# Token tiles handed from one part of a network to the next in a written-out order

## The chip, the cores and the metric

The kernel runs on one core of a Trainium2 chip. The metric is the device time of one execution, in microseconds (us). A core has a matrix engine (PE, with its weight loads as PEld), a vector engine (DVE), a scalar engine (ACT), a general engine (POOL) and an engine that only issues transfers (SP). Each engine runs its own instructions in the order in which they stand in its stream, and waits on semaphores for the others.

## The reference

Two layers, each of three parts; x is 512 tokens by 1024 channels, in float32:

```
x = x + 0.5 * rms(FFN1(rms(x) * g_pre)) * g_post     # SwiGLU, width 2816
x = x +       rms(MIXER(rms(x) * g_pre)) * g_post    # attention + convolution + linear attention, gated, projected
x = x + 0.5 * rms(FFN2(rms(x) * g_pre)) * g_post
```

So there are six parts, and five times the output of one part, still in the accumulators, has to be normed, scaled by `g_post`, added to x, normed again, scaled by `g_pre` and transposed before the next part can multiply with it. This passage is what the change touches.

## The kernel before, in words

Tokens are tiled by 128 into four tiles. Every product is made from three matmuls, because each operand is split into a high part (rounded by ACT, `hi` or `h`) and a low part (the difference, by DVE, `lo` or `l`): high x high, high x low, low x high. `split` (line 111) is that pair; the weights are loaded by SP into `raw` and split into `whi` and `wlo` (lines 112 and 113, of which there are five buffers each).

An FFN multiplies by seven half-size products instead of eight (`block_tiles`, then `Down` for the down projection). `Down.run` (line 614) goes through its products step by step, with weights asked for four steps ahead; after the third product it calls `late` (line 640), which fetches the next two norm weights, `g_post` of this part and `g_pre` of the next (`load_g`, line 188: one row broadcast to 128 partitions, 512 KB).

`out_proj` (line 258) ends every part. All but the last four steps of the contraction are accumulated for all tokens first. The last four (`rest`) are then run token tile by token tile: token 0, 1, 2, 24 matmuls of 512 columns each, and token 3. Two accumulators, one for each half of the channels, are thus complete after each 12 matmuls. After each token `finish` is called. It runs `post_norm` (line 239), that is

- for an FFN, `Down.results` (line 657), which adds or subtracts the taps kept from the seven products;
- `rms` (line 197): two squares with a sum on ACT, a mean on DVE (`ms`), a power on POOL (`rs`);
- two scalings by `g_post` on DVE (`tn`, line 244), which free the accumulators, and two adds to x (line 248);

and `pre_norm` (line 210): `rms` again, on x, then two scalings by `rs` and `g_pre` into `hn` on DVE (line 220). For tiles 0 and 1 the second half is instead multiplied by `g_pre` on POOL (line 214) and scaled by `rs` on ACT (line 218).

`pre_norm` returns `arrive`, which is called later: eight transposes on PE (line 71), a split into `xh` and `xl` (lines 112, 113), and before an FFN the copies `xr` and the sums and differences T that the seven products need. Tile 0's `arrive` is called after the first quarter of token 3's matmuls. Those of tiles 1 to 3 are called by the next part: in the middle of the product of the tile before (mixer, `pv`, line 780) or between its gate and up halves (FFN, `pf`, lines 701 to 705).

`early` fetches the first weights of the next part in four steps. The first step is taken before token 0, the other three after token 3's matmuls are written. The mixer's first product takes two of its eight contraction blocks from each step; the FFN's gate takes the first two steps and its up half the other two.

What sets the order: matmuls and transposes are pinned, and so is all of `block_tiles` and `Down`. A pinned instruction (`tc.keep_in_program_order`, line 68) stays behind everything that the program wrote before it on its engine. Everything else is placed by a planner, which picks what it takes to be ready, earlier lines first. In the kernel before all of `post_norm`, `pre_norm`, `arrive`, the early weights' splits and `load_g` are left to the planner.

Of the kernel before, what the change touches and what calls it, by code (L numbers as in the profile page):

```python
# [13 lines left out]
P = 128  # L14
D = 1024
# [26 lines left out]
def kernel(  # L42
# [58 lines left out]
    def room(n, dt=F32R):  # L101
        cur[n] = resid.tile([P, KC, S], dt, tag=n, name=n)
        return cur[n]
# [4 lines left out]
        nc.sync.dma_start(x_sb[i], x_in[0, i * P:(i + 1) * P, :])  # L108


    def split(hi, lo, src):
        nc.scalar.copy(hi, src)  # L112
        nc.vector.tensor_tensor(lo, src, hi.bitcast(F32), op=ALU.subtract)  # L113

    spare = []

# [70 lines left out]

    def load_g(row):
        g = gp.tile([P, D], F32, tag="g", name="g")
        nc.sync.dma_start(g, row.unsqueeze(0).broadcast_to([P, D]))  # L190
        return g

    def rsqrt_eps(dst, src, n):
# [16 lines left out]
    def pre_norm(i, gB, pooled=(), forms=None):  # L210
        t = slice(i * P, (i + 1) * P)
        hns = [slot("hn", tag="b") for j in range(2)]
        for j in pooled:
            nc.gpsimd.tensor_tensor(hns[j], x_sb[i][:, HS[j]], gB[:, HS[j]], op=ALU.mult)
        rs = rms([x_sb[i][:, c] for c in HS])
        for j in range(2):
            if j in pooled:
                nc.scalar.mul(hns[j], hns[j], rs)
            else:
                nc.vector.scalar_tensor_tensor(hns[j], x_sb[i][:, HS[j]], rs, gB[:, HS[j]], op0=ALU.mult, op1=ALU.mult)  # L220

        def arrive():
            if i == 0:
                room("xh")
                room("xl")
            pts = []
            for j, hn in enumerate(hns):
                pt = bank("pt")
                for k in range(4):
                    transpose(pt[:, k * P:(k + 1) * P], hn[:, k * P:(k + 1) * P], ident)  # L230
                src = pt.rearrange("p (k t) -> p k t", t=P)
                split(cur["xh"][:, 4 * j:4 * j + 4, t], cur["xl"][:, 4 * j:4 * j + 4, t], src)
                pts.append(src)
            if forms is not None:
                forms.arrive(i, pts)

        return arrive

    def post_norm(i, banks, gB, factor):
        rs = rms(banks)  # L240
        tn = []
        for h in range(2):
            t = slot("tn", tag="s")
            nc.vector.scalar_tensor_tensor(t, banks[h], factor, gB[:, HS[h]], op0=ALU.mult, op1=ALU.mult)
            tn.append(t)
        for h in range(2):
            x = x_sb[i][:, HS[h]]
            nc.vector.scalar_tensor_tensor(x, tn[h], rs, x, op0=ALU.mult, op1=ALU.add)  # L248

    def load_rows(w2d, k):  # L250
        return load_w([(lambda r: r, w2d[k * P:(k + 1) * P, :])], 1024)
# [6 lines left out]
    def out_proj(w2d, nk, stat, tail, finish, upcoming, early, head=None):  # L258


        ld = lambda k: load_rows(w2d, k)
        fresh = head is None
        if fresh:
            banks = [[bank(f"o{i}{h}", "pb" if i < 3 else "pa") for h in range(2)] for i in range(NT)]
        else:
            banks, rest = head

        def mms(i, h, k, sh, sl, wh, wl):
            mm_out(banks[i][h], slice(i * P, (i + 1) * P), sh, sl, wh[:, HS[h]], wl[:, HS[h]],
                   fresh and k == 0, k == nk - 1)  # L270

        for k in range(nk - tail if fresh else 0):
            wh, wl = ld(k)
            sh, sl = stat(k)
            for i in range(NT):
                for h in range(2):
                    mms(i, h, k, sh, sl, wh, wl)
        if fresh:
            rest = [(k, ld(k), stat(k)) for k in range(nk - tail, nk)]
        w = None  # L280
        if early is not None:
            w, steps = early()
            next(steps)
        for i in range(NT - 1):
            for h in range(2):
                for k, (wh, wl), (sh, sl) in rest:
                    mms(i, h, k, sh, sl, wh, wl)
            finish(i, banks[i])

        for n, (k, (wh, wl), (sh, sl)) in enumerate(rest):  # L290
            for h in range(2):
                mms(NT - 1, h, k, sh, sl, wh, wl)
            if upcoming and n == tail // 2 - 2:
                upcoming[0]()
        if w is not None:
            for _ in steps:
                pass
        finish(NT - 1, banks[NT - 1])
        return w


# [178 lines left out]
    class Down:  # L480
# [173 lines left out]
                rest.append((self.steps[p][1], (hi, lo), (sh, sl)))  # L654
            return self.out, rest

        def results(self, i, banks):

            tt = nc.vector.tensor_tensor
            if i >= 2:  # L660
                tt(self.p1[i - 2], banks[0], self.p1[i - 2], op=ALU.add)
                return [self.p1[i - 2], banks[1]]
            tt(self.u2[i], banks[0], self.u2[i], op=ALU.subtract)
            tt(self.u4[i], banks[1], self.u4[i], op=ALU.add)
            return [self.u2[i], self.u4[i]]


    def ffn_weights(wg, wu):
# [12 lines left out]
    def ffn(wg, wu, wd, weights, forms, arrive, finish, upcoming, early, late, begin):  # L681

        if begin is None:
            wgt, wut = weights
        else:
            wgt = load_kcols(wg, 0, 256)
            begin(0)
            wut = load_kcols(wu, 0, 256)
            begin(1)
            arrive[0]()  # L690
        hk = []
        hid = [None] * NF

        def silu_up(i, pf):
            h = slot("ht", tag="s")
            nc.scalar.activation(h[:, 0:256], pf[:, 0:256], AF.Silu)
            nc.vector.tensor_tensor(h[:, 0:256], pf[:, 256:512], h[:, 0:256], op=ALU.mult)
            hk.append(h)

        for i in range(NT):  # L700
            pf = bank("pf", "pb")
            mm_tok(pf[:, 0:256], i, wgt)
            if i + 1 < NT:
                arrive[i + 1]()
            mm_tok(pf[:, 256:512], i, wut, first=False)
            if i + 1 < NT:
                silu_up(i, pf)

        pts = []

        def between(g):

            if g == -6:
                sides.append(load_cols(wg, 2 * P))
                forms.finish("T3")
            if g == -5:
                silu_up(NT - 1, pf)
                sides.append(load_cols(wu, 2 * P))
                pg = bank("pg")
                mm_cols(pg, *sides[0])  # L720
                for f in range(2):
                    pt = bank("pth", "pa")
                    for i in range(NT):
                        transpose(pt[:, i * P:(i + 1) * P], hk[i][:, f * P:(f + 1) * P], ident)
                    pts.append(pt)
                pu = bank("pu")
                mm_cols(pu, *sides[1])
                pts.extend((pg, pu))
            if g == -4:
                forms.finish("T2")  # L730
            if g == -2:
                forms.finish("T1")
                for f in range(2):
                    hid[f] = slot("hid", tag="q")
                    pinned(nc.scalar.copy(hid[f], pts[f]))
            if g == -1:
                hid[2] = slot("hid")
                pinned(nc.scalar.activation(hid[2], pts[2], AF.Silu))
            if g == 0:
                forms.finish("T4")  # L740
            if g == 1:
                pinned(nc.vector.tensor_tensor(hid[2], pts[3], hid[2], op=ALU.mult))
                for f in range(3, NF):
                    hid[f] = slot("hid", tag="t" if f < 18 else "q")
                down.pairs()

            u, j = divmod(g, 7)
            if j in (2, 4) and u > 0:
                down.sum_tokens(fs[u - 1], j // 4)
            if g in (n - 5, n - 3, n - 1):  # L750
                down.ahead()

        sides = []
        spare.clear()
        fs = list(range(3, NF))
        n = 7 * len(fs)
        down = Down(wd, hid)
        block_tiles(wg, wu, fs, forms, hid, between)
        head = down.run(late)
        return out_proj(wd, NF, None, TAIL, lambda i, b: finish(i, down.results(i, b)), upcoming, early, head)  # L760


    def mixer(l, wv, arrive, finish, upcoming, early):
# [521 lines left out]
    for idx, (l, s) in enumerate(subs):  # L1285
# [10 lines left out]
        here, forms = forms, Forms() if s != 0 else None  # L1296
        ahead = forms

        def finish(i, banks, ahead=ahead):
            post_norm(i, banks, norms[0], 1.0 if s == 1 else 0.5)  # L1300
            if len(norms) > 1:
                upcoming.append(pre_norm(i, norms[1], (1,) if i < 2 else (), ahead))
            else:
                for h in range(2):
                    nc.sync.dma_start(out[0, i * P:(i + 1) * P, HS[h]], x_sb[i][:, HS[h]])

        early = None
        if idx + 1 < len(subs):
# [40 lines left out]
```

## Time and profile before

| | us |
|---|---|
| median of three runs | 2348.26 (2348.12 to 2349.34) |
| the profiled execution | 2348.53 |
| its span, first to last instruction | 2346.8 |
| PE busy | 2314.0 |
| DVE busy | 1850.4 |
| ACT busy | 1225.1 |
| POOL busy | 178.4 |

In the profile's rows, `out<-in` names what an instruction writes and reads, by the program's names; `L112` is line 112. A row of instructions has its start, its length and, in brackets, the idle time of its engine just before it and what ended that. A matmul's end is modelled: one of 512 columns is shown 0.39 long, though the next is issued 0.23 later. `c`, `o` and the like are the accumulators: `oA` to `oD` of the down projection, `o` of the mixer's output, `pv` and `pf` of the next part's first product. The granted clock is the share of full speed at which PE was let run.

### The profile page before, as it was taken

The page shows a single profiled execution, that of the slowest core. Times are in us where ns is not written, and L with a number is a line of the kernel's source. Part 1 is how long each engine was busy: PE and PEld are TensorE (multiplying, and loading weights), DVE is VectorE, ACT ScalarE, POOL GpSimd, SP SyncE. Part 2 cuts the span into 40 slices and gives each one's busy share as a digit, 9 for nine tenths or more (in the row PEclk, how much of TensorE's full clock was granted, in tenths as well). Part 3 has the DMA queues.
Part 4 walks back from the last instruction along what each step waited for, and adds up shares of the span by engine and source line. Part 5 has one row for each costly group of instructions (what it writes and reads, how often), then busy time and mean ns, then how long its engine had stood idle before and what let it go on. Part 6 is the DMA issues. An engine that isn't in the chain of part 4 may idle for free. (4 is left out here: it accounts for less than half of the span.)

```text
span 2346.8 us, 36172 instructions
## 1 busy us (share of the span) xinstructions
PE 2314.0 (99%) x14072; PEld 2060.0 (88%) x14072; DVE 1850.4 (79%) x2745; ACT 1225.1 (52%) x2380; POOL 178.4 (8%) x287
## 2 busy tenths in 40 slices
PE   8999999999999999999999999999999999999998
PEld 7999887887888899997899997788878888999977
DVE  7888987859975388889788889778599644888896
ACT  5565655644323265566555566566433233565663
POOL 0000001211021100000000000012010211000000
PEclk9999999999999999999999999999999999999999
DMA  5333643231333223336423336441413322333462
GB/s 172 93 107 109 215 161 110 63 94 55 109 90 101 88 73 106 100 101 222 155 74 108 109 117 219 132 118 54 113 45 101 107 90 81 89 100 101 129 213 98
DMA packets 332764, 265.33 MB, mean 113 GB/s; under 512 B 12746, under 2 KB 285164, under 8 KB 332592
## 3 DMA queue, kind: packets, MB, share of 16 engines
q1 hardware_dynamic: 332592, 263.02, 36.8%
q8 instruction: 110, 1.80, 0.3%
q14 instruction: 62, 0.51, 0.1%
HBM read 260.88 MB, written 2.10 MB: 112 GB/s over the span
## 5 line engine op out<-in xcount | busy, mean ns | idle before, releaser
L366 DVE TENSOR_TENSOR wlo<-raw,whi 128x1024 fp32r<-128x1024 f32 (+1 forms) x304 | 331.2, 1089 | 108.7 <-ACT whi L364 108.0
L364 ACT CAST whi<-raw 128x512 fp32r<-128x512 f32 x532 | 315.4, 620 | 160.1 <-DVE raw L366 160.1
L112 ACT CAST whi<-raw 128x1024 fp32r<-128x1024 f32 (+2 forms) x178 | 185.5, 1045 | 353.2 <-PE gate L66 131.0
L113 DVE TENSOR_TENSOR wlo<-raw,whi 128x1024 fp32r<-128x1024 f32 (+2 forms) x178 | 223.1, 1262 | 168.7 <-ACT whi L112 161.9
L366 DVE TENSOR_TENSOR raw<-raw 128x512 f32<-128x512 f32 x304 | 209.3, 689 | 5.8
L66 PE MATMUL A<-xh,whi 128*128 128x256 f32 x608 | 172.5, 284 | 0.0
L66 PE MATMUL A<-xh,wlo 128*128 128x256 f32 x608 | 172.0, 283 | 0.0
L66 PE MATMUL A<-xl,whi 128*128 128x256 f32 x608 | 172.0, 283 | 0.0
L939 DVE SCALAR_TENSOR_TENSOR y<-u,cw,y 128x511 f32<-128x511 f32 (+14 forms) x240 | 166.8, 756 | 0.0
L579 ACT CAST whi<-raw 128x1024 fp32r<-128x1024 f32 x104 | 109.6, 1053 | 81.1 <-issue 36.0
L66 PE MATMUL gate<-xh,whi 128*128 128x512 f32 x384 | 151.3, 394 | 0.0
L66 PE MATMUL gate<-xh,wlo 128*128 128x512 f32 x384 | 149.8, 390 | 1.3 <-DVE wlo L113 1.3
L66 PE MATMUL gate<-xl,whi 128*128 128x512 f32 x384 | 149.6, 390 | 0.0
L582 DVE TENSOR_TENSOR wlo<-raw,whi 128x1024 fp32r<-128x1024 f32 x104 | 127.8, 1229 | 24.8 <-ACT whi L579 24.8
L205 POOL TENSOR_TENSOR rs<-ms,mhalf 128x1 f32<-128x1 f32 x48 | 28.2, 587 | 1441.2 <-DVE ms L203 1441.2
L66 PE MATMUL oA<-wlo,dh 128*128 128x512 f32 x304 | 119.7, 394 | 7.0 <-DVE wlo L582 7.0
L364 ACT COPY cp<-A 128x256 f32<-128x256 f32 x228 | 84.5, 370 | 70.6 <-PE A L66 69.7
L66 PE MATMUL oA<-whi,dl 128*128 128x512 f32 x304 | 118.4, 390 | 0.0
L66 PE MATMUL oA<-whi,dh 128*128 128x512 f32 x304 | 118.4, 389 | 0.0
L66 PEld LDWEIGHTS A<-xl,whi 128*128 128x128 f32 x608 | 116.6, 192 | 0.2
L66 PEld LDWEIGHTS A<-xh,whi 128*128 128x128 f32 x608 | 116.5, 192 | 0.2
L66 PEld LDWEIGHTS A<-xh,wlo 128*128 128x128 f32 x608 | 116.6, 192 | 0.0
(326 smaller groups left out, 7116.6 us busy)
## 6 DMA issues: line engine op xcount, KB each, us to landing
raw<-in_ffn_w_down_dram SPq DMA_DIRECT2D x152, 512.0 KB, 4.6
raw<-in_w_in_dram SPq DMA_DIRECT2D x108, 512.0 KB, 4.6
raw<-in_ffn_w_gate_dram SPq DMA_DIRECT2D x152, 256.0 KB, 3.4
raw<-in_ffn_w_up_dram SPq DMA_DIRECT2D x152, 256.0 KB, 4.5
raw<-in_w_branch_dram SPq DMA_DIRECT2D x24, 512.0 KB, 3.6
raw<-in_w_out_dram SPq DMA_DIRECT2D x16, 512.0 KB, 4.0
raw<-in_ffn_w_gate_dram SPq DMA_DIRECT2D x12, 512.0 KB, 4.9
raw<-in_ffn_w_up_dram SPq DMA_DIRECT2D x12, 512.0 KB, 4.6
```

The costliest lines, as they stand in the source:

```text
L66: tc.keep_in_program_order(nc.tensor.matmul(*a, **k))
L112: nc.scalar.copy(hi, src)
L113: nc.vector.tensor_tensor(lo, src, hi.bitcast(F32), op=ALU.subtract)
L205: nc.gpsimd.tensor_tensor(rs, ms, mhalf[:, 0:1], op=ALU.pow)
L364: copy = lambda o, i: pin(nc.scalar.copy(o, i))
L366: tt = lambda o, a, b, op: pin(nc.vector.tensor_tensor(o, a, b, op=op))
L579: pinned(nc.scalar.copy(hi, src))
L582: pinned(nc.vector.tensor_tensor(lo, src, hi.bitcast(F32), op=ALU.subtract))
L939: nc.vector.scalar_tensor_tensor(y[:, back:], u[:, :S - back], cw[:, c, j:j + 1], y[:, back:], op0=ALU.mult, op1=ALU.add)
```

## The change

1. `post_norm` and `pre_norm` of the handing-over are replaced by a class `Hand`, one object per token tile, whose steps (`sum`, `square`, `mean`, `scaled`, `add`, `normal`) are called one by one from `out_proj`. Every step on ACT and DVE is pinned; POOL's power isn't. All normals are made on DVE; POOL's multiply and ACT's scaling go.
2. `out_proj` spells the order out for tiles a, b, c, d, between the matmuls of tokens 0 to 3. Tile 0's `arrival` now stands ahead of all of token 3's matmuls. While `held` is set, `split` is pinned too: tile 0's, and those of the four early weight steps. The first step still stands before token 0; the second now stands after tile c's add and its squares, the third after d's squares, the fourth after d's scalings.
3. The next part's call for tile 1 becomes `second`: tile 1's arrival, then d's add, mean and normals. Tiles 2 and 3 follow as before.
4. `load_g` is pinned: the fetch stays behind every transfer written before it. In an FFN that is behind the weights asked for up to the last step of the third product.
5. The last part, which hands nothing on, runs the same steps tile by tile, pinned.

```diff
+    held = [False]
+
     def split(hi, lo, src):
-        nc.scalar.copy(hi, src)
-        nc.vector.tensor_tensor(lo, src, hi.bitcast(F32), op=ALU.subtract)
+        pin = pinned if held[0] else lambda x: x
+        pin(nc.scalar.copy(hi, src))
+        pin(nc.vector.tensor_tensor(lo, src, hi.bitcast(F32), op=ALU.subtract))
...
-        nc.sync.dma_start(g, row.unsqueeze(0).broadcast_to([P, D]))
+        pinned(nc.sync.dma_start(g, row.unsqueeze(0).broadcast_to([P, D])))
...
+    class Hand:
...
+        def square(self, h, second=False):
+            if h == 0:
+                self.ss = sm.tile([P, 2], F32, tag="ss", name="ss")
+            pinned(nc.scalar.activation(junk, self.x(h) if second else self.src[h], AF.Square, scale=1.0 / 32.0,
+                                        accum_out=self.ss[:, h:h + 1]))
+        def mean(self):
+            ms = sm.tile([P, 1], F32, tag="ms", name="ms")
+            pinned(nc.vector.tensor_scalar(ms, self.ss[:, 0:1], self.ss[:, 1:2], EPS, op0=ALU.add, op1=ALU.add))
+            self.rs = sm.tile([P, 1], F32, tag="rs", name="rs")
+            nc.gpsimd.tensor_tensor(self.rs, ms, mhalf[:, 0:1], op=ALU.pow)
...
+        def half(self, h):
+            self.sum(h)
+            self.square(h)
+            self.scaled(h)
+        def add(self):
+            for h in range(2):
+                pinned(nc.vector.scalar_tensor_tensor(self.x(h), self.tn[h], self.rs, self.x(h),
+                                                      op0=ALU.mult, op1=ALU.add))
+            for h in range(2 if self.gpre is not None else 0):
+                self.square(h, True)
+        def normal(self):
+            self.hns += [slot("hn", tag="b") for h in range(2)]
+            for h, hn in enumerate(self.hns):
+                pinned(nc.vector.scalar_tensor_tensor(hn, self.x(h), self.rs, self.gpre[:, HS[h]],
+                                                      op0=ALU.mult, op1=ALU.mult))
...
+        held[0] = True
+        a, b, c, d = [finish(i, banks[i]) for i in range(NT)]
+        forms = finish(None, None)
+        w, steps = early()
+        next(steps)
+        token(0)
+        a.half(0)
+        a.half(1)
+        a.mean()
+        token(1)
+        a.add()
+        b.half(0)
+        a.mean()
+        b.sum(1)
+        a.normal()
+        b.square(1)
+        b.scaled(1)
+        b.mean()
+        token(2)
+        c.half(0)
+        b.add()
+        c.half(1)
+        b.mean()
+        c.mean()
+        b.normal()
+        arrival(0, a.hns, forms)
+
+        for k, (wh, wl), (sh, sl) in rest:
             for h in range(2):
                 mms(NT - 1, h, k, sh, sl, wh, wl)
-            if upcoming and n == tail // 2 - 2:
-                upcoming[0]()
-        if w is not None:
-            for _ in steps:
-                pass
-        finish(NT - 1, banks[NT - 1])
+        c.add()
+        next(steps)
+        c.mean()
+        d.sum(0)
+        d.sum(1)
+        d.square(0)
+        d.square(1)
+        next(steps)
+        d.scaled(0)
+        d.scaled(1)
+        for _ in steps:
+            pass
+        d.mean()
+        c.normal()
+        held[0] = False
+
+        def second():
+            arrival(1, b.hns, forms)
+            d.add()
+            d.mean()
+            d.normal()
+
+        upcoming.extend((None, second, lambda: arrival(2, c.hns, forms), lambda: arrival(3, d.hns, forms)))
         return w
```

`Down.sum` is `Down.results` for one half, pinned; `scaled` is the scaling by `g_post`, pinned; `arrival` is the old `arrive`, unchanged.

More of the change, by code (lines that the diff above doesn't have):

```diff
@@ L220, in pre_norm @@
                 nc.vector.scalar_tensor_tensor(hns[j], x_sb[i][:, HS[j]], rs, gB[:, HS[j]], op0=ALU.mult, op1=ALU.mult)
[L222 to L248, printed above, removed]
+        return lambda: arrival(i, hns, forms)
@@ new lines, in arrival @@
+    def arrival(i, hns, forms):
+        t = slice(i * P, (i + 1) * P)
+        if i == 0:
+            room("xh")
+            room("xl")
+        pts = []
+        for j, hn in enumerate(hns):
+            pt = bank("pt")
+            for k in range(4):
+                transpose(pt[:, k * P:(k + 1) * P], hn[:, k * P:(k + 1) * P], ident)
+            src = pt.rearrange("p (k t) -> p k t", t=P)
+            split(cur["xh"][:, 4 * j:4 * j + 4, t], cur["xl"][:, 4 * j:4 * j + 4, t], src)
+            pts.append(src)
+        if forms is not None:
+            forms.arrive(i, pts)
@@ new lines, with __init__, x, sum @@
+    class Hand:
+        def __init__(self, i, banks, sums, gpost, gpre, factor):
+            self.i, self.banks, self.sums, self.gpost, self.gpre, self.factor = i, banks, sums, gpost, gpre, factor
+            self.src, self.tn, self.hns = list(banks), [None, None], []
+        def x(self, h):
+            return x_sb[self.i][:, HS[h]]
+        def sum(self, h):
+            if self.sums is not None:
+                self.src[h] = self.sums(self.i, h, self.banks[h])
+        def square(self, h, second=False):
[8 more added lines that the diff above has]
+            nc.gpsimd.tensor_tensor(self.rs, ms, mhalf[:, 0:1], op=ALU.pow)
+        def scaled(self, h):
+            self.tn[h] = slot("tn", tag="s")
+            pinned(nc.vector.scalar_tensor_tensor(self.tn[h], self.src[h], self.factor, self.gpost[:, HS[h]],
+                                                  op0=ALU.mult, op1=ALU.mult))
[13 more added lines that the diff above has]
+                pinned(nc.vector.scalar_tensor_tensor(hn, self.x(h), self.rs, self.gpre[:, HS[h]],
+                                                      op0=ALU.mult, op1=ALU.mult))
@@ L279, in out_proj, with token @@
             rest = [(k, ld(k), stat(k)) for k in range(nk - tail, nk)]
[L280 to L284, printed above, removed]
+        def token(i):
             for h in range(2):
@@ L287, in out_proj @@
                     mms(i, h, k, sh, sl, wh, wl)
-            finish(i, banks[i])
-        for n, (k, (wh, wl), (sh, sl)) in enumerate(rest):
+        if early is None:
+            for i in range(NT):
+                token(i)
+                finish(i, banks[i])
+            return None
+        held[0] = True
[25 more added lines that the diff above has]
+        for k, (wh, wl), (sh, sl) in rest:
             for h in range(2):
                 mms(NT - 1, h, k, sh, sl, wh, wl)
-            if upcoming and n == tail // 2 - 2:
-                upcoming[0]()
-        if w is not None:
-            for _ in steps:
-                pass
-        finish(NT - 1, banks[NT - 1])
+        c.add()
[19 more added lines that the diff above has]
+        upcoming.extend((None, second, lambda: arrival(2, c.hns, forms), lambda: arrival(3, d.hns, forms)))
         return w
@@ L655, in run, with sum @@
             return self.out, rest
-        def results(self, i, banks):
-            tt = nc.vector.tensor_tensor
-            if i >= 2:
[L661 to L665, printed above, removed]
+        def sum(self, i, h, bank_):
+            tt = lambda o, a, b, op: pinned(nc.vector.tensor_tensor(o, a, b, op=op))
+            if i >= 2 and h == 0:
+                tt(self.p1[i - 2], bank_, self.p1[i - 2], ALU.add)
+                return self.p1[i - 2]
+            if i >= 2:
+                return bank_
+            o = (self.u2 if h == 0 else self.u4)[i]
+            tt(o, bank_, o, ALU.subtract if h == 0 else ALU.add)
+            return o
     def ffn_weights(wg, wu):
@@ L759, in ffn @@
         head = down.run(late)
-        return out_proj(wd, NF, None, TAIL, lambda i, b: finish(i, down.results(i, b)), upcoming, early, head)
+        return out_proj(wd, NF, None, TAIL, lambda i, b: finish(i, b, down.sum), upcoming, early, head)
     def mixer(l, wv, arrive, finish, upcoming, early):
@@ L1297, with finish @@
         ahead = forms
-        def finish(i, banks, ahead=ahead):
-            post_norm(i, banks, norms[0], 1.0 if s == 1 else 0.5)
+        def finish(i, banks, sums=None, ahead=ahead):
+            if i is None:
+                return ahead
+            hand = Hand(i, banks, sums, norms[0], norms[1] if len(norms) > 1 else None, 1.0 if s == 1 else 0.5)
             if len(norms) > 1:
[L1302 to L1305, printed above, removed]
+                return hand
+            hand.half(0)
+            hand.half(1)
+            hand.mean()
+            hand.add()
+            for h in range(2):
+                nc.sync.dma_start(out[0, i * P:(i + 1) * P, HS[h]], x_sb[i][:, HS[h]])
         early = None
```

## The prediction

> **What bounds the kernel now.** First the page's head, for the span and the shares.
>
> ```profile
> span 2346.8 us, 36172 instructions
> PE 2314.0 (99%) x14072; PEld 2060.0 (88%) x14072; DVE 1850.4 (79%) x2745; ACT 1225.1 (52%) x2380; POOL 178.4 (8%) x287
> ```
>
> PE is busy all but 33 us of the span, so whatever the change does must show in what PE waits for. That view comes next (waiter, releaser, total us, times, longest).
>
> ```profile
> PE oA L66 <- DVE wlo L582: 7.0, 12, 0.6
> PE pf L66 <- ACT xh L112: 3.0, 2, 1.7
> PE pv L66 <- ACT xh L112: 2.6, 2, 1.3
> PE pf L66 <- DVE xl L113: 1.6, 3, 0.6
> PE pv L66 <- DVE xl L113: 1.5, 3, 0.8
> ```
>
> The first line is the down projection, short of DVE; the other four are what the change is about, PE's first products of a part waiting for a token tile (part of pf's is the start of the program). Third, busy time by stretch: the five hand-overs between parts, each from the first matmul of token 0 in the old part to the last of tile 3 in the new one, and then five windows of 3.41 us around two of them (columns: stretch, length, PE, PEld, DVE, ACT, POOL busy with counts, granted PE clock, DMA share, GB/s).
>
> ```profile
> 333.98:385.03 51.05, 49.35 (x225) 40.16 (x223) 37.32 (x58) 26.95 (x56) 6.98 (x10) 0.97 0.30 84
> 810.47:859.05 48.58, 48.52 (x321) 44.51 (x320) 37.55 (x68) 28.93 (x60) 7.80 (x10) 1.00 0.25 66
> 1153.32:1206.27 52.95, 50.57 (x321) 46.01 (x320) 42.93 (x74) 28.08 (x59) 6.97 (x10) 0.97 0.22 61
> 1499.97:1550.57 50.60, 48.16 (x225) 38.89 (x224) 37.22 (x58) 26.86 (x56) 6.97 (x10) 1.00 0.30 85
> 1976.00:2024.58 48.58, 48.52 (x321) 44.51 (x320) 37.55 (x68) 28.93 (x60) 7.80 (x10) 1.00 0.24 66
> 356.12:359.53 3.41, 1.71 (x6) 0.81 (x6) 3.41 (x6) 2.66 (x7) 0.15 (x1) 1.00 0.01 2
> 359.53:362.95 3.42, 3.42 (x9) 2.65 (x8) 3.36 (x5) 2.48 (x3) 0.39 (x1) 0.50 0.99 262
> 1175.32:1178.73 3.41, 1.48 (x7) 0.81 (x6) 3.37 (x6) 2.52 (x8) 0.02 (x2) 1.00 0.01 2
> 1520.07:1523.48 3.41, 2.71 (x12) 1.90 (x11) 2.70 (x6) 2.53 (x7) 0.55 (x1) 1.00 0.00 0
> 1523.48:1526.90 3.42, 2.43 (x9) 1.72 (x10) 3.35 (x6) 3.42 (x7) 0.55 (x1) 1.00 0.28 65
> ```
>
> Order of the hand-overs: FFN to mixer, mixer to FFN, FFN to FFN, FFN to mixer, mixer to FFN. A 512-column matmul is issued every 0.227 us and a half-clock one every 0.427 us:
>
> ```profile
> 356.18 0.39 PE L66 MATMUL oA<-wlo,dh 128*128 128x512 f32 x1
> 356.41 0.39 PE L66 MATMUL oA<-whi,dl 128*128 128x512 f32 x1
> 358.12 0.50 PE L66 MATMUL pv<-whi,xh 128*128 128x512 f32 x1 [1.32 <-ACT xh L112]
> 360.01 0.63 PE L66 MATMUL pv<-wlo,xh 128*128 128x512 f32 x1
> 360.44 0.63 PE L66 MATMUL pv<-whi,xl 128*128 128x512 f32 x1
> ```
>
> 256 columns take 0.120 and a tile's eight transposes 0.87, as two pieces of the chain that ended last show:
>
> ```profile
> 2008.63 0.87 PE pt L71 x8
> 2016.12 8.63 PE pf L66 x72
> ```
>
> So a hand-over to the mixer needs 192 x 0.227 + 4 x 0.87 = 47.0, and one to an FFN 96 x 0.227 + 192 x 0.120 + 4 x 0.87 = 48.3. Above that floor lie 4.0, 0.3, 4.7, 3.6 and 0.3 us: 12.9 in all, the most that the change can win here. Of it 1.6 twice is clock: after windows in which PE was busy 1.71 and 1.48 of 3.41, the next ran at 0.50 (8 matmuls x 0.20); after 2.71 and 2.43 none did. So PE idle for 1.7 of a window cost the clock, idle for 1.0 did not.
>
> **What the change does to PE's wait.** Why tile 0 is late is in ACT's and DVE's order around 357 (start, us).
>
> ```profile
> 351.10 0.63 ACT L201 ACTIVATE junk<-x 128x512 bf16<-128x512 f32 x1
> 351.86 0.63 ACT L201 ACTIVATE junk<-p 128x512 bf16<-128x512 f32 x1
> 354.94 1.04 ACT L112 CAST whi<-raw 128x1024 fp32r<-128x1024 f32 x1
> 357.50 0.56 ACT L112 CAST xh<-pt 128x512 fp32r<-128x512 f32 x1
> 359.06 2.95 ACT L112 CAST whi<-raw 128x1024 fp32r<-128x1024 f32 x3
> 355.21 0.68 DVE L244 SCALAR_TENSOR_TENSOR tn<-oA,g 128x512 f32<-128x512 f32 x1
> 356.02 1.42 DVE L248 SCALAR_TENSOR_TENSOR x<-tn,rs,x 128x512 f32<-128x512 f32 x2
> 361.29 2.35 DVE L113 TENSOR_TENSOR wlo<-raw,whi 128x1024 fp32r<-128x1024 f32 x2
> ```
>
> Tile 0 is transposed in the middle of token 3, but its copy stands on ACT behind token 2's squares on x. The change puts all eight transposes ahead of token 3 and their copies right behind token 2's first squares. That wait goes. What is late next is the new part's weights, in four steps W1 to W4 (a copy on ACT, a difference on DVE). The old order copies W2 at 354.94 and W3, W4 from 359.06. The new one holds W2 behind token 2's add and its two squares, W3 behind token 3's two squares, W4's difference behind token 3's two scalings. ACT and DVE run in order, so everything traced later queues behind: tile 1's copies and the clearing of the banks.
>
> Per-step prices, from these rows (the two-row entries give the pitch: 0.67 for an add, and for a normal, which is the same kind of instruction, 1.13 for a difference, 0.95 for a copy; squares follow each other by 0.76):
>
> ```profile
> L113 DVE TENSOR_TENSOR wlo<-raw,whi 128x1024 fp32r<-128x1024 f32 x8 | 9.7, 1222 | 2.5 <-ACT whi L112 2.2
> L113 DVE TENSOR_TENSOR xl<-pt,xh 128x512 fp32r<-128x512 f32 x8 | 5.3, 684 | 2.1 <-ACT xh L112 2.1
> L205 POOL TENSOR_TENSOR rs<-ms,mhalf 128x1 f32<-128x1 f32 x8 | 4.4, 550 | 337.5 <-DVE ms L203 337.5
> ```
>
> *FFN to mixer, in the clock of the first.* Token 2's banks are done at 333.98 + 72 x 0.227 + 0.2 = 350.5. From there DVE runs its scaling (0.69), tile 1's mean, waits for POOL's power (0.55) until 352.4, makes tile 1's two normals (to 353.8), tile 0's two low parts (to 355.0) and token 2's two adds (to 356.3). ACT squares them to 357.1, copies W2 to 358.1; DVE subtracts to 359.4. Then DVE sums token 3 to 360.1, ACT squares twice to 361.6, copies W3 to 362.6, DVE W3 to 363.9, two scalings, W4 to 366.2, one mean, tile 2's normals, tile 1's low part at 368.3.
> PE ends token 3 at 356.6 and starts tile 0 at once. It wants W2 at 358.0, waits 0.2 for the copy and 1.04 for the difference; tile 1's transposes; waits 1.2 + 1.04 for W3, 1.0 for W4, 0.5 + 0.2 for low parts. Sum 5.1 above the floor, where it was 4.0 and 3.6: **+1.1 and +1.5**.
> *FFN to FFN:* the same chain; the gate half takes W1, W2 (24 x 0.12), the up half W3, W4. Waits 0.1 + 1.1, 1.0 + 1.1, 0.9, 0.5 = 4.9 against 4.7: **+0.2**.
> *Mixer to FFN:* no sums in front of the squares, so W3 comes in time; W2 waits 1.0, W4 0.9, tile 1's low part 0.5: 2.4 against 0.3: **+2.1 twice**.
> Sum **+7.1 us**. Every price in it is measured; unknown is the slack between engines, about 0.1 per change of engine on some eight changes: +-0.8 for each hand-over, +-4 in all.
>
> *The clock.* The new waits stand close: 1.2 + 1.04 within 2.5 us, fed by FFNs. Inside one window that is about 1.9 idle after the 0.16 by which each modelled matmul end lies later than its issue. By the windows above that is over the mark, and where windows fall is not in the kernel's hand. A half-clock window costs between 0 (it falls into the wait for W4) and 1.6 (as now). I take 0.5 for each of three: **+1.5**, ends 0 and +4.8. The Trainium skill ("TensorE: Matmul & The Clock Gate", section on HAM oscillation) gives "no PE-idle gaps >~3.4µs" as the abstract rule; by it none of these waits would touch the clock. The trace contradicts it, at 1.70 idle of 3.41 in two pieces.
>
> **The norm weights' fetch.** SP's queue in the first FFN; DVE's wait for down weights over all four FFNs; and the same wait in the last one alone (us, times, longest):
>
> ```profile
> 237.67 0.47 SPq L190 DMA_DIRECT2D g<-in_norm_post_dram  x1
> 246.13 0.35 SPq L190 DMA_DIRECT2D g<-in_norm_pre_dram  x1
> 247.27 11.56 SPq L124 DMA_DIRECT2D raw<-in_ffn_w_down_dram  x10
> L552 DVE TENSOR_TENSOR xh<-raw 128x1024 f32<-128x1024 f32 x16 | 19.5, 1220 | 8.2 <-DMA raw<-in_ffn_w_down_dram 8.2
> DVE xh L552 <- DMA raw<-in_ffn_w_down_dram: 1.7, 1, 1.7
> ```
>
> Both fetches (512 KB each) now ride between down-projection weights; the second is right ahead of a batch for which DVE later waits 8.2 us over four FFNs. Pinned behind the loads that the third product's last step asks for, they move on by up to 12 x 12 x 0.227 = 33 us. There the loads run four steps, 11 us, ahead of their products, which covers two fetches: no cost; without that cover each would cost the 0.5 us of its issue and its share of the transfer. The gain ends at the 7.0 of PE's down waits, should the fetch cause them all, and at 0, should it cause none: what DVE waits for is down weights, not g. The fetch is one of eleven transfers there, so I take a tenth, **-0.7**; it is nearer the end at 0.
>
> **At nothing.** POOL's multiply and ACT's scaling for tiles 0 and 1 go, DVE makes those halves (0.75, in the chain above). The last part hands nothing on: its final sum, square, scale, mean, add keep their order, cover or none. At the start the fetch already follows the first x.
>
> Sum on the profiled execution, 2348.53 (span 2346.8 and 1.7 around it): + 7.1 + 1.5 - 0.7 = 2356.4. The median of the runs, 2348.26, lies 0.3 below it: **2356**.
>
> **Rivals.**
> *B, a clean hand-over.* W2 to W4 are not what PE waits for; only tile 0's wait counted. For it: four of PE's waits name xh and xl, none wlo there. Against: those waits hid the weights, whose W3 and W4 were subtracted only by 361.29 + 2.35 = 363.6. All 12.9 above the floor and 0.7 go: 2335.
> *C, a draw.* The fetch is what starves the down projection, and its move wins the whole 7.0: 7.1 + 1.5 - 7.0 = +1.6, time 2350. For it: the fetch lands on the batch that DVE waits for. Against: the last FFN of the program has no second fetch and still waits 1.7, against a mean of 2.05.
> *D, no half clock* (the page's rule would give the same): waits as in the sum, but the window falls between them: 2355. Two windows of 1.0 idle did not lose the clock.
> *E, worse.* The part's fifth weight copy is not held; put on DVE ahead of token 2's adds it shifts each chain by 1.13: 5 x 1.13 = 5.7 more, 2362. For it: its bytes are there. Against: DVE has no idle time there before 356.
>
> **How the numbers follow.** Forecast 0.38, D 0.24, C 0.18, B 0.13, E 0.07. Range 2344 to 2362: it leaves out B and a little above E. The forecast with D alone: 2351 to 2361. A measurement can tell 0.2%, 4.7 us, from no change: faster is B and an edge of C, 0.15; slower (over 2353) most of the forecast, D and E, 0.61; the rest 0.24.
>
> **What would show it.** Right: xh gone from PE's waits at the hand-overs, pv and pf waiting for whi L112 and wlo L113 in its place; hand-overs of 52 to 53 us out of an FFN and 51 out of the mixer; ACT's copy of W2 behind two squares on x, after token 3. DVE's wait on down weights a little under 8.2. Wrong: hand-overs near 47 and 48; or tile 1's transposes or the bank clearing waited for, which I cost at nothing.

## The result, and the profile after

The changed kernel takes 2360.87 us (median of four runs, 2360.26 to 2361.50), the kernel before 2348.21 beside it: 1.0053 times as long, 95% interval 1.0035 to 1.0070. It is slower, by 12.7 us where 8 were forecast, and inside the forecast's range.

The head of the changed kernel's page:

```profile
span 2359.8 us, 36148 instructions
PE 2318.9 (98%) x14072; PEld 2063.6 (87%) x14072; DVE 1850.6 (78%) x2755; ACT 1219.3 (52%) x2370; POOL 165.8 (7%) x277
```

The span grew by 13.0 us. Next, what PE waits for (waiter, releaser, total us, times, longest):

```profile
PE oA L66 <- DVE wlo L670: 5.5, 10, 0.6
PE pf L66 <- ACT whi L115: 4.1, 3, 1.4
PE pv L66 <- DVE wlo L116: 4.0, 6, 0.8
PE pv L66 <- ACT whi L115: 4.0, 3, 1.7
PE pf L66 <- DVE wlo L116: 3.9, 5, 0.9
PE pf L66 <- ACT xh L115: 1.9, 1, 1.9
PE pf L66 <- DVE xl L116: 0.8, 2, 0.6
PE oC L66 <- DVE wlo L670: 0.6, 1, 0.6
```

What pv and pf wait for has changed its name. Tile 0's `xh` is gone (the 1.9 that is left is the program's start), and the next part's weights stand there: 16.0 us for `whi` and `wlo`, none before. The down projection's waits on `oA` and `oC` fell from 7.8 to 6.1.

The five hand-overs, cut as before, and then windows of 3.41 us around their waits (stretch, length, PE, PEld, DVE, ACT, POOL busy with counts, granted PE clock, DMA share, GB/s):

```profile
333.59:387.12 53.53, 50.19 (x226) 40.20 (x224) 36.85 (x60) 25.68 (x54) 4.73 (x8) 0.97 0.29 80
812.55:864.91 52.36, 49.30 (x321) 44.69 (x320) 38.57 (x70) 28.22 (x58) 4.73 (x8) 1.00 0.23 61
1158.20:1213.00 54.80, 51.91 (x322) 47.16 (x321) 42.49 (x76) 26.94 (x57) 4.74 (x8) 0.94 0.21 59
1504.94:1558.78 53.84, 48.93 (x226) 38.97 (x224) 36.77 (x60) 25.70 (x54) 4.73 (x8) 1.00 0.29 80
1984.18:2036.82 52.64, 50.37 (x321) 46.16 (x320) 38.58 (x70) 28.00 (x58) 4.73 (x8) 0.97 0.23 61
356.99:360.40 3.41, 1.28 (x5) 0.50 (x3) 1.53 (x3) 2.09 (x5) 0.00 (x0) 1.00 0.00 0
360.40:363.82 3.42, 3.39 (x11) 2.82 (x12) 0.92 (x3) 2.60 (x6) 0.55 (x1) 0.50 0.67 185
1527.76:1531.17 3.41, 1.75 (x7) 0.96 (x6) 1.53 (x3) 2.38 (x5) 0.00 (x0) 1.00 0.00 0
1531.17:1534.59 3.42, 2.40 (x14) 1.80 (x13) 1.53 (x3) 1.76 (x5) 0.55 (x1) 1.00 0.37 95
```

Their sum is 267.2 us, 28.3 above the floors (two of 47.0, three of 48.3), where it was 12.9: +15.4. Summed over the four down projections, what the matmuls' spacing exceeds its usual value by fell from 11.9 to 9.3 us: -2.6. That leaves 0.2 of the 13.0 for everything else.

Where the time goes in a hand-over, in the first of them (timeline, rows picked: start, us):

```profile
349.57 0.63 ACT L261 ACTIVATE junk<-x 128x512 bf16<-128x512 f32 x1 [0.66 <-DVE x L282]
350.32 0.63 ACT L261 ACTIVATE junk<-x 128x512 bf16<-128x512 f32 x1
351.07 0.60 ACT L261 ACTIVATE junk<-oA 128x512 bf16<-128x512 f32 x1
351.80 0.69 DVE L272 SCALAR_TENSOR_TENSOR tn<-oA,g 128x512 f32<-128x512 f32 x1 [1.66 <-ACT junk L261]
353.34 0.75 DVE L290 SCALAR_TENSOR_TENSOR hn<-x,rs,g 128x512 f32<-128x512 f32 x1 [0.61 <-POOL rs L268]
355.87 1.40 DVE L282 SCALAR_TENSOR_TENSOR x<-tn,rs,x 128x512 f32<-128x512 f32 x2
356.70 0.63 ACT L261 ACTIVATE junk<-x 128x512 bf16<-128x512 f32 x1 [3.98 <-DVE x L282]
358.09 1.03 ACT L115 CAST whi<-raw 128x1024 fp32r<-128x1024 f32 x1
359.15 1.23 DVE L116 TENSOR_TENSOR wlo<-raw,whi 128x1024 fp32r<-128x1024 f32 x1 [1.88 <-ACT whi L115]
359.17 0.50 PE L66 MATMUL pv<-whi,xh 128*128 128x512 f32 x1 [1.40 <-ACT whi L115]
360.43 0.80 PE L66 MATMUL pv<-wlo,xh 128*128 128x512 f32 x1 [0.76 <-DVE wlo L116]
```

Read it from below. PE stops at 357.6 for the second weight step's copy, which ACT makes at 358.09 behind the squares on x, those wait for token 2's adds (355.87), and these stand in DVE's queue behind the scaling at 351.80. That scaling reads an accumulator that PE had finished at about 350.1. DVE idled 1.66 us, until ACT had squared the same accumulator; and ACT did so only after two squares on x.

### The profile page after: what moved, and what is told of

It reads as the page before. It is cut to its first block, busy times and chain, and to the rows that moved or that the text cites. A ratio compares the mean times of both kernels' runs of the same rounds, so it can differ in the third digit from the quotient of the medians.

```text
span 2359.8 us, 36148 instructions
## 1 busy us (share of the span) xinstructions
PE 2318.9 (98%) x14072; PEld 2063.6 (87%) x14072; DVE 1850.6 (78%) x2755; ACT 1219.3 (52%) x2370; POOL 165.8 (7%) x277
## 4 chain that ended last, share of the span: by engine, by line
PE 89%; DVE 6%; ACT 1%; DMA 1%; issue 1%; POOL 0%; SPq 0%; DVEq 0%; POOLq 0%; ACTq 0%
PE A L66 18%; PE gate L66 11%; PE C L66 9%; PE pb L66 6%; PE oA L66 5%; PE B L66 5%; PE pf L66 4%; PE o L66 3%; PE oC L66 3%; PE oB L66 3%; PE gr L66 2%; PE pa L66 2%; PE q L66 2%; PE gv L66 2%; PE pgl L66 2%; PE k L66 2%
```

## The experiments

Above the floors means, here and below, the five hand-overs' sum less 238.9. "Sum worked out by hand" means the held order laid end to end with the prediction's durations.

**1. The fetch alone, and the hand-over alone.** First the kernel before with one line changed, then the changed kernel without it:

```diff
-        nc.sync.dma_start(g, row.unsqueeze(0).broadcast_to([P, D]))
+        pinned(nc.sync.dma_start(g, row.unsqueeze(0).broadcast_to([P, D])))
```

> The kernel before with one edit, the norm weights' fetch held behind the third product's loads. Theory of the prediction, corrected by the changed kernel's profile: the fetch did cost the down projection, whose waits for wlo fell from 7.8 to 5.9 us and whose whole excess over the nominal pitch fell from 11.9 to 9.3, so 2348.2 - 2.6 = 2345.6. The prediction's own term, a tenth of the wait: 2347.5. Rival: those 2.6 us come from the other rhythm that the new hand-over gives the loads, or from chance, and the fetch alone changes nothing: 2348.2.

> The changed kernel with the fetch of the norm weights let go again, as before. If the fetch is worth 2.6 us: 2360.9 + 2.6 = 2363.5, and the five hand-overs stay 28 us above their floors. If the gain in the down projection belongs to the hand-over's order: 2360.9.

Measured: the fetch alone 2345.45 (2344.36 to 2347.78) against 2348.66, ratio 0.9986 (0.9977 to 0.9996), a gain of 3 us. The hand-over alone 2365.24 (2363.28 to 2367.53), ratio 1.0068 (1.0053 to 1.0083), 28.6 above the floors; 2363.5 was expected. DVE's wait for down weights (us, times, longest), in the changed kernel, with the fetch alone and with the hand-over alone:

```profile
DVE xh L640 <- DMA raw<-in_ffn_w_down_dram: 5.4, 5, 2.7
```

```profile
DVE xh L552 <- DMA raw<-in_ffn_w_down_dram: 5.6, 5, 2.1
```

```profile
DVE xh L640 <- DMA raw<-in_ffn_w_down_dram: 8.1, 6, 2.0
```

The wait follows the fetch and not the hand-over: 5.4 and 5.6 with the fetch held, 8.1 and 8.2 without. The fetch alone makes the kernel faster; the rewritten hand-over costs more than that.

**2. Which of the two fetches.** The first try held only the fetch of `g_pre`, with `g_post`'s left free and written ahead of it.

```diff
-                norms.append(load_g(norm_pre[subs[idx + 1][0], subs[idx + 1][1]]))
+                norms.append(load_g(norm_pre[subs[idx + 1][0], subs[idx + 1][1]], pinned))
```

> The kernel before with only the fetch of the next part's weights (g_pre) held behind the third product's loads; the fetch of g_post stays where it was. Theory: the g_pre fetch, issued 2.0 us into the down projection and 1.1 us ahead of the batch of weights that DVE waits for, is what delays that batch, by about 1.1 us in each of three FFNs: 2348.5 - 2.9 = 2345.6, as with both held, and DVE's wait for down weights falls in the first three FFNs and stays near 1.7 in the last. Rival: the g_post fetch, 6.4 us ahead of the down projection, is the one that matters: 2348.5.

Measured 2348.49 (2347.59 to 2351.02), ratio 0.9999 (0.9989 to 1.0008). But every engine's order stayed that of the kernel before, so this run tells nothing about the fetch (DVE's wait, 8.7 against 8.2, shows how far it scatters with nothing moved). It tells how far a hold reaches. The result fits a hold that ties one instruction to the one written just before it on its engine, and no further. `g_pre`'s fetch was tied to `g_post`'s, and `g_post`'s was free. (That a pinned instruction stays behind everything written before it, as the description ahead of the prediction has it, is true only where the instruction before is itself in its place.) The second try wrote the two apart, `late(False)` for `g_post`, free, and `late(True)` for `g_pre`, held:

```diff
             while self.next < self.AHEAD:
                 self.ahead()
+            late(False)
...
-                    late()
+                    late(True)
```

> The kernel before with the two fetches written apart: g_post's behind the first four steps' loads, where it stood, and only g_pre's held behind the third product's loads. (In the run that held g_pre alone behind g_post the order of the queue did not change, so it said nothing.) The planner also orders the mixer's work a little differently here, so the rows count, not the last us. Theory: the g_pre fetch ahead of the batch costs DVE about 1.1 us in each of three FFNs; DVE's wait for down weights falls from 8.2 to about 5 (near 0.6, 1.4, 1.0 and still 1.7 in the last), and the time is near 2345.6. Rival: g_post is the one that matters, or both together: the wait stays at 7 to 8, time 2348.5.

Measured 2345.50 (2344.33 to 2347.12), ratio 0.9988 (0.9978 to 0.9997), and of DVE's wait:

```profile
DVE xh L552 <- DMA raw<-in_ffn_w_down_dram: 5.5, 6, 1.7
```

`g_post` was fetched 6.4 us ahead of the first down product as before, `g_pre` some 28 us behind it instead of 2.0, and the wait fell just as far as with both held. SP's order is the only one that differs from the kernel before. So `g_pre`'s fetch, ahead of the batch, is what delayed it. In the second FFN both traces show a load of that batch land: it is issued 3.1 us behind the first down product in both, and lands 7.9 us behind it with the fetch ahead, 6.7 without. By FFN the waits were 2.1, 1.3, 0.4 and 1.7 (before 1.8, 2.6, 2.1 and 1.7): the sum is clear, a single FFN scatters by half a us or more, and the last, which has no such fetch, kept its wait.

**3. Who reads an accumulator first.**

```diff
         def half(self, h):
             self.sum(h)
-            self.square(h)
             self.scaled(h)
+            self.square(h)
...
-        b.square(1)
         b.scaled(1)
+        b.square(1)
```

> The changed kernel with the scaling of an accumulator on DVE written ahead of its square on ACT (half, and tile b's second half); nothing else is moved. Theory 1: of two engines that read one accumulator the one written second waits for the first. In the changed kernel DVE's scaling of tile c's second half stood 1.66 us behind ACT's square, which stood behind tile b's squares on x, and with it DVE's whole queue. With the order turned, c's adds come 1.4 us earlier out of an FFN and 1.7 out of the mixer, and the five hand-overs' sum above the floors falls from 28 to 20.5: 2360.9 - 7.6 = 2353.3. ACT's squares of raw accumulators should now start behind DVE's scalings. Theory 2: the waits are longer than predicted through slack at each change of engine; then the order of the two readers changes nothing: 2360.9.

Measured 2354.05 (2352.06 to 2355.76), ratio 1.0021 (1.0012 to 1.0030); 21.1 above the floors (52.27, 50.76, 53.70, 52.52, 50.76), where the hand sum gives 20.5. The same place in its timeline:

```profile
350.82 0.69 DVE L272 SCALAR_TENSOR_TENSOR tn<-oA,g 128x512 f32<-128x512 f32 x1
351.03 0.63 ACT L261 ACTIVATE junk<-x 128x512 bf16<-128x512 f32 x1
351.78 0.60 ACT L261 ACTIVATE junk<-oA 128x512 bf16<-128x512 f32 x1
352.72 1.41 DVE L290 SCALAR_TENSOR_TENSOR hn<-x,rs,g 128x512 f32<-128x512 f32 x2
```

DVE's scaling no longer waits. Counted from each hand-over's start (334.30 here, 333.59 above), the normals come at 18.4 instead of 19.75, 1.3 us earlier; c's adds come 1.3 us earlier out of an FFN and 1.6 out of the mixer. Theory 1 holds. The Trainium skill has the reason ("PSUM — Partial Sum Buffer", section "PSUM bank collisions raise a hardware error"): two engines must not touch the same bank of the accumulators at one time, two readers included, and the compiler's scheduler puts a dependency between them. The waits here agree with it; no run let two engines read one bank together.

**4. The weights' place.**

```diff
+        for _ in steps:
+            pass
         c.add()
-        next(steps)
         c.mean()
...
-        next(steps)
         d.scaled(0)
         d.scaled(1)
-        for _ in steps:
-            pass
```

> The changed kernel with the early weights' steps 2, 3 and 4 moved ahead of tile c's adds, all three right behind tile 0's arrival. Theory: at the hand-overs PE waits for the weights because of where their steps stand. Then whi and wlo go from PE's waits in pv and pf; what is late next is tile 1, whose copies on ACT stand behind tile c's and d's squares: waits of about 1.1 to 2.0 for xh and 1.9 to 2.1 for xl at tile 1's first matmuls, five hand-overs at 18 above the floors instead of 28: 2360.9 - 10 = 2351. Rival: the weights' place is not what PE waits for (their buffers come free only with token 3's matmuls, so the copies can't start earlier): no change, 2360.9.

Measured 2342.28 (2340.40 to 2343.14), ratio 0.9970 (0.9957 to 0.9982): faster than the kernel before, and far faster than expected; 9.5 above the floors (48.63, 49.96, 50.54, 49.08, 50.18). What PE waits for in it at the hand-overs:

```profile
PE pt L71 <- DVE hn L290: 3.5, 4, 1.4
PE pf L66 <- DVE wlo L116: 2.6, 3, 0.9
```

`whi` is gone, and of `wlo` 0.9 is left three times. The expected waits for tile 1 did not come. ACT in the first hand-over:

```profile
358.80 0.63 ACT L261 ACTIVATE junk<-x 128x512 bf16<-128x512 f32 x1 [2.61 <-DVE x L282]
359.44 0.57 ACT L115 CAST xh<-pt 128x512 fp32r<-128x512 f32 x1
359.90 0.63 ACT L261 ACTIVATE junk<-x 128x512 bf16<-128x512 f32 x1
360.53 0.57 ACT L115 CAST xh<-pt 128x512 fp32r<-128x512 f32 x1
361.93 0.63 ACT L261 ACTIVATE junk<-p 128x512 bf16<-128x512 f32 x1 [0.82 <-DVE p L745]
```

Tile 1's copies are not held, and the planner set them between c's squares, ahead of d's. I had laid them behind. That this is why no wait came is read from the rows; no run held these copies with the weights in this place.

**5. Both.** Edits 3 and 4 together.

> The changed kernel with both edits: scalings ahead of squares, and the weights' steps 2 to 4 ahead of c's adds. Theory: the two causes are apart and add up. The 0.9 us that is left at wlo in three hand-overs with the weights first goes, since b's normals come earlier, and tile 2's transposes wait 0.7 us less for c's normals: the sum above the floors goes from about 10 (weights first) to 4.4, time 2342.3 - 5.5 = 2337. Rival: the two edits win the same time twice; then it stays near 2342.

Measured 2334.62 (2333.06 to 2335.78), ratio 0.9938 (0.9921 to 0.9954): 14 us faster than the kernel before. The hand-overs, and what PE still waits for there:

```profile
333.07:380.26 47.19, 47.19 (x226) 39.16 (x224) 37.04 (x60) 25.85 (x54) 5.25 (x8) 1.00 0.34 91
805.67:853.98 48.31, 48.31 (x321) 44.45 (x320) 38.34 (x70) 27.84 (x58) 5.18 (x8) 1.00 0.25 66
1147.67:1197.50 49.83, 48.66 (x321) 44.46 (x320) 41.99 (x75) 26.31 (x56) 5.25 (x8) 1.00 0.24 64
1490.47:1537.79 47.32, 47.32 (x225) 39.16 (x223) 36.89 (x60) 25.64 (x54) 5.25 (x8) 1.00 0.34 91
1963.20:2011.52 48.32, 48.32 (x321) 44.45 (x320) 38.34 (x70) 27.83 (x58) 5.19 (x8) 1.00 0.24 66
```

```profile
PE pt L71 <- DVE hn L290: 1.1, 1, 1.1
```

2.1 above the floors (4.4 expected); four of five stand at them. The two causes add up: alone they took 7.2 and 18.8 off the 28.3, together 26.2.

**6. Another order, all held.** Tile b's normals behind c's adds, d's work behind tile 1's arrival, d's last mean and normals behind tile 2's, and those tiles' copies held as well; square ahead of scaling as in the changed kernel.

```diff
-        b.normal()
         arrival(0, a.hns, forms)
...
+        next(steps)
+        next(steps)
         c.add()
+        b.normal()
         c.mean()
         d.sum(0)
+        for _ in steps:
+            pass
...
+        def third():
+            arrival(2, c.hns, forms)
+            d.mean()
+            d.normal()
```

> The changed kernel with the same steps in another held order: weight steps 2 and 3 right behind tile 0's arrival, then c's adds, b's normals, c's mean, d's first sum, weight step 4; the rest of d and c's normals behind tile 1's arrival, d's last mean and normals behind tile 2's, and the copies of tiles 1 and 2 held there too. Theory: what costs is the place of a few steps, not that an order is held. Laid end to end with the traced durations, and with the rule that the second reader of an accumulator waits for the first, the five hand-overs come to 1.4 us above their floors instead of 28: 2360.9 - 26.7 = 2334.2. Rival: a held order is rigid, and small lags at each change of engine add up in it; then about 5 us above the floors of slack for eight changes of engine in each of five hand-overs stay: 2338. Worse rival: held copies of tiles 1 and 2 block ACT's queue in front of the squares: 2345 or more.

> As the reordered kernel, but the copies and differences of tiles 1 and 2 are left to the planner. If they land where the held order has them: 2334, the same. If the planner puts them behind d's squares: waits of about 1 us at tile 1 in each hand-over, 2339.

Measured 2348.32 (2346.50 to 2349.98), ratio 0.9997 (0.9988 to 1.0007), and with the copies left to the planner 2347.60 (2344.49 to 2348.85), ratio 0.9993 (0.9984 to 1.0003): no gain, where 14 us were expected. Into a mixer the order does what was laid out (47.54 and 47.76). Into an FFN it does not (53.80, 52.27, 53.74). What is late there, on DVE and PE at the second hand-over:

```profile
846.14 0.76 DVE L429 TENSOR_TENSOR T<-T,xr 128x256 f32<-128x256 f32 x2
846.82 0.20 DVE L266 TENSOR_SCALAR ms<-ss 128x1 f32<-128x1 f32 x1
847.76 1.41 DVE L290 SCALAR_TENSOR_TENSOR hn<-x,rs,g 128x512 f32<-128x512 f32 x2 [0.73 <-POOL rs L268]
```

```profile
848.66 0.52 PE L71 MATMUL pt<-ident,hn 128*128 128x128 f32 x3 [2.00 <-DVE hn L290]
```

Before an FFN an arrival also writes the sums and differences T on DVE. d's mean, held behind tile 2's arrival, stands behind all of them, and tile 3's transposes wait 2.0 us in each of the three hand-overs. The order was laid without the T's. (This cause is read from the rows; no run moved d's mean.)

The clock adds to it. Nothing is waited for behind tile 3's transposes, so a half-clock window that falls there is paid in full. The two hand-overs out of the mixer lost one (granted clock 0.97: 53.80 and 53.74), the one between the FFNs did not (1.00: 52.27). With the copies left to the planner the waits are as long, but the window moved from the first hand-over out of the mixer to the one between the FFNs, and the time moved with it:

```profile
805.32:857.67 52.35, 49.44 (x322) 44.46 (x320) 38.93 (x70) 28.29 (x58) 4.73 (x8) 1.00 0.22 61
1151.33:1205.08 53.75, 50.92 (x321) 45.93 (x320) 42.82 (x76) 27.03 (x57) 4.74 (x8) 0.97 0.22 60
```

So a window costs 1.5 us here. Holding the copies or not made no difference to the waits, so it is not the held copies that block; and the excess stands in the hand-overs into an FFN alone, not in all five as small lags would. Neither rival is what happened.

## Why the prediction was right, and where it was off

- *What bounds, and what is late next:* right. `xh` left the hand-overs' waits, the weights took its place, ACT copies W2 behind the two squares on x with token 3 already over, and the hand-overs out of an FFN and out of the mixer all grew. Putting the weights' steps earlier took away 18.8 of the 28.3: shown.
- *The waits' size:* too small, +7.1 (with the clock +8.6) where +15.4 was measured. The step that failed is "From there DVE runs its scaling (0.69)", from 350.5 on: I took a scaling to be free as soon as PE has finished the accumulator. It waits for ACT's square of the same accumulator. In the third experiment, where it does not, the prediction's chain holds nearly as it was laid: the hand-overs stand 5.3, 2.5, 5.4, 5.5 and 2.5 above their floors, where it had 5.1, 2.4, 4.9, 5.1 and 2.4, and the sum is 21.1 against 12.9 + 7.1 = 20.0. The 1.3 us out of an FFN and 1.6 out of the mixer that this experiment won back, added to the 20.0, give 27.1; measured 28.3. (The waits that the prediction lists from FFN to FFN add up to 4.7, not 4.9; that changes little.) The trace of before had it in the open, in the mixer's hand-over on DVE, and on ACT:

```profile
814.11 0.69 DVE L244 SCALAR_TENSOR_TENSOR tn<-o,g 128x512 f32<-128x512 f32 x1 [1.13 <-ACT junk L201]
```

```profile
813.39 0.60 ACT L201 ACTIVATE junk<-o 128x512 bf16<-128x512 f32 x1 [1.67 <-PE o L66]
813.88 0.19 ACT L201 ACTIVATION_READ_ACCUMULATOR junk<-o 128x1 f32 x1
```

  The scaling starts 0.04 after the square's end (813.88 + 0.19). There it cost nothing, as that hand-over stood 0.3 above its floor; the new order put ACT's squares on x in front of it. I priced slack between engines at +-0.8 for each hand-over; this was 1.3 to 1.6, on one side in all five.
- *The clock:* +1.5 was taken, about nothing came. Three of the five hand-overs did run at 0.50, the number I used, one of them for two windows on end. But the hand-overs of one kind do not differ by it: into the mixer 53.53 with such a window and 53.84 without, out of it 52.64 with and 52.36 without. With the hand-over alone all five had one or two, and the sum was 28.6. The slow matmuls fall into the time until the next weight step comes, which was the lower end of my range. The upper end, "1.6 (as now)", was wrong for the kernel before too, and its own rows show it: the two hand-overs into the mixer took 51.05 with such a window and 50.60 without, 0.45 apart. With the fetch alone the one from FFN to FFN kept its clock and took 52.91, against 52.95 with the window. The mark is not a sharp one: a window with PE busy 1.75 kept the clock here, two with 1.76 and 1.77 lost it. So rival D, no half clock, was wrong in what happens and right that the clock's price is not in the time.
- *The norm weights' fetch:* -0.7 was taken, -2.6 measured in the down projection and 3 us alone. The step that failed is "one of eleven transfers there, so I take a tenth". Its place was right, ahead of the batch that DVE waits for. Its size was not: the wait of three FFNs fell by 2.7 in all when it alone was moved. The argument from the last FFN, which has no such fetch and still waits 1.7, showed only that most of the wait is not the fetch's. Rival C, all 7.0, took it for everything: 2.6 is between.
- *At nothing:* the last part kept its steps, and nothing of tile 1's transposes was waited for. What the hand-overs and the down projection leave of the difference is 0.2 us.
- *Rival B*, the clean hand-over at 2335, was wrong for this change, since the weights are what PE waits for; with the weights' steps and the two readers put in the right order it is 2334.6. *Rival E* did not happen, though its 2362 is the nearest number: the trace shows no weight difference on DVE between the scaling at 351.80 and the adds at 355.87.
- *Luck:* the range held in part because two errors have opposite signs. The waits with the clock were 6.8 too low, the fetch's gain 1.9 too small. With the forecast's 0.7 for the fetch the same waits give 2362.8, past the range's end at 2362, and the hand-over alone measured 2365.24.

## What to carry to other kernels

When an order is written out by hand, each step takes everything behind it on its engine with it. So list all that a step issues (the T sums of an arrival were forgotten in the sixth experiment), and set first what the engine that must not wait needs next, here the weights and not the following token tile. Two engines that read one accumulator follow each other in the order written: let the one whose queue is free read first. Not everything has to be held: in the fourth experiment the planner placed tile 1's copies better than I had laid them.

## What was not expected of the hardware

A half-clock window has no fixed price. Where PE had to wait for data behind it, it cost little or nothing: two pairs of like hand-overs, with and without it, lie 0.3 us apart with opposite signs in the changed kernel, and 0.45 in the kernel before. Where no wait followed, in the sixth experiment, it cost 1.5 us (53.80 and 52.35 for the same hand-over). And a single fetch of 512 KB, issued 1.1 us ahead of a batch of weights in the same queue, made that batch late, by 1.2 us where its landing shows; DVE's wait for it over three FFNs was 2.7 us longer in all, unevenly, though it was one of eleven transfers.
